# Decoder layer on one core: the second product of both FFNs by one level of Strassen's method, chained in PSUM

## The chip, the cores and the metric

The kernel runs on one core of one Trainium2 chip. The metric is the device time of one execution in microseconds (us), the median over several runs; lower is better. All inputs and the output are float32 in DRAM, and one launch computes the whole layer.

## The reference

One layer on a sequence of 512 tokens of width 1024: two SwiGLU FFNs with a hidden width of 2816, a token mixing between them (HGRN2 heads and causal pooling), a cross-attention into 256 memory tokens, and a layer norm after each of the four. What the change touches is the product with `w_out`:

```python
def _layernorm(x, g, b):
    ...
    return ((xf - mu) * lax.rsqrt(var + LN_EPS) * g + b)

def _swiglu(h, w_in, w_out):
    gate, up = jnp.split(h @ w_in, 2, axis=-1)      # w_in [1024, 5632]
    return (jax.nn.silu(gate) * up) @ w_out         # w_out [2816, 1024]

h = _layernorm(ALPHA * h + 0.5 * _swiglu(h, w_ffn1_in, w_ffn1_out), ln1_g, ln1_b)
h = _layernorm(ALPHA * h + _parallel_mixer(h, ...), ln2_g, ln2_b)
h = _layernorm(ALPHA * h + _memory_attention(h, mem, ...), ln3_g, ln3_b)
h = _layernorm(ALPHA * h + 0.5 * _swiglu(h, w_ffn2_in, w_ffn2_out), ln4_g, ln4_b)
```

## The kernel before

**Arithmetic.** Every large product is taken three times. An operand is split into two exact parts of type float32r, hi and lo: ScalarE (ACT) writes hi with a cast (L59), VectorE (DVE) subtracts it from the source and writes lo (L60). `mm3` (L53 to 56) then adds hi·hi, hi·lo and lo·hi in one PSUM bank. So a weight block of 128x1024 costs one DMA of 512 KB (L65), one cast of 128x1024 on ACT, one subtraction of 128x1024 on DVE, and its matmuls on TensorE (PE). Of the three matmuls on a tile the third is the first that reads the weight's lo part in `proj_T`; in the token-major products it is the second.

**Memory.** A DMA lands in `raw`, a ring of 3 buffers of the pool `wp`. The split halves of a weight go to the tags `whi` and `wlo` of the same pool, 4 buffers each (L70, L71), which nothing else uses but the first loads of x. The pool `big` has 15 slots of 8 KB per partition (`b8`, L44), which hold the activations; the last 4 weight blocks of an output product also go there (`stay`, L67). PSUM has 6 banks `mm` and 2 banks `tr`.

**First product of an FFN** (`ffn`, L239 to 265). It is feature-major: for each of the 22 column tiles j, `proj_T` (L220) makes the gate `pg` and the value `pu`, each [128 columns, 512 tokens], by 8x3 matmuls of 128x512. `glu` takes Silu of `pg` on ACT (L244), multiplies by `pu` from PSUM on DVE (L245) and splits the product into the tiles `f1g`/`f2g` (L247). Where a phase starts with the output of a layer norm, `proj_T2` (L228) makes two column tiles in halves of 256 tokens, so that the first half can start before the last tokens are normed.

**Second product** (`out_gemm`, L171 to 217). It is token-major: for each half of 512 output columns (hf) and each of 4 token tiles (t), 22 contraction tiles x 3 matmuls of 128x512 (L191 to 193) go into one PSUM bank: 2x4x22x3 = 528 matmuls for each FFN. The last blocks of a half are kept so that the token tiles end one after another. Then DVE adds the bank to the residual `h` (L204), takes the statistics (L207), and `ln_tile` (L141) norms the tile: bn_aggr (L144), variance plus eps (L146), a power on GpSimd (POOL, L148), and four DVE passes over 128x512 (L151, L154). `transpose_h` (L158) turns the normed tile by 8 PE transposes `trh`, and ACT and DVE split the result into the tiles `f1T` for the next phase.

**Order of the work.** Tile places the instructions of the program on each engine's queue, and each engine works through its queue in order. A tile of a pool can be written once the last reader of its slot is done, so the sizes of the pools decide how far ahead of its use on PE a weight's cast and subtraction stand in the queues of ACT and DVE. SyncE (SP) issues all DMAs.

Of the kernel before, what the change touches and what calls it, by code (L numbers as in the profile page):

```python
# [9 lines left out]
F32 = mybir.dt.float32  # L10
# [6 lines left out]
P = 128  # L17
# [6 lines left out]
H = 4  # L24
# [9 lines left out]
def layer_kernel(ctx: ExitStack, tc: tile.TileContext, a, out):  # L34
    nc = tc.nc
    const = ctx.enter_context(tc.tile_pool(name="const", bufs=1))
    big = ctx.enter_context(tc.tile_pool(name="big", bufs=15))
    wp = ctx.enter_context(tc.tile_pool(name="wp", bufs=4))
    res = ctx.enter_context(tc.tile_pool(name="res", bufs=1))
# [23 lines left out]
    def wblock(src, name, stay=False):  # L63
        raw = wp.tile([P, 1024], F32, tag="raw", name=f"raw_{name}", bufs=3)
        nc.sync.dma_start(raw, src)  # L65
# [19 lines left out]
    for k in range(KT):  # L85
# [3 lines left out]
        hi = wp.tile([P, 512], F32R, tag="whi", name=f"whix{k}")  # L89
        lo = wp.tile([P, 512], F32R, tag="wlo", name=f"wlox{k}")  # L90
# [25 lines left out]
    # lower bound of the forget gate: softmax over the two rows, first row  # L116
# [17 lines left out]
    def ln_bcast(g, b):  # L134
        G = sm.tile([P, D], F32, tag="G", name="G", bufs=1)
        B = sm.tile([P, D], F32, tag="B", name="B", bufs=1)
# [34 lines left out]
    def out_gemm(wsrc, nkt, act, alpha, g, b, eps, name, final=False, order=None, head0=None):  # L171
# [7 lines left out]
        for hf in range(2):  # L179
# [19 lines left out]
            ws = [wblock(wsrc[hf, order[i]], f"{name}{hf}_{i}", stay=hf == 1) for i in range(head, nb)]  # L199
# [28 lines left out]
    def proj_T2(ws, X, name):  # L228
        """Two column tiles at the start of a phase: the first half of the tokens goes first."""
# [8 lines left out]

    def ffn(win, wout, X, g, b, name, final, first=None):  # L239
        gt = [b8([P, 2, 2, S], F32R, f"{name}g{q}") for q in range(FT // 2)]  # L240

        def glu(j, pg, pu):
            sg = sm.tile([P, S], F32, tag="sg", name=f"{name}sg")
            nc.scalar.activation(sg, pg, AF.Silu)  # L244
            nc.vector.tensor_tensor(out=sg, in0=sg, in1=pu, op=ALU.mult)  # L245
            T = gt[j // 2]
            split(sg, T[:, j % 2, 0, :], T[:, j % 2, 1, :])  # L247

        j0 = 0
        if first is not None:  # L250
            for j, (pg, pu) in enumerate(first):
                glu(j, pg, pu)
            j0 = len(first)
        for j in range(j0, FT):
            ws = [wblock(win[j], f"{name}g{j}"), wblock(win[FT + j], f"{name}u{j}")]
            if j == 0:
                pg, pu = proj_T2(ws, X, f"{name}p")
            else:
                pg = proj_T(ws[0], X, name=f"{name}pg")
                pu = proj_T(ws[1], X, name=f"{name}pu")  # L260
            glu(j, pg, pu)
            if first is not None and 4 <= j < 4 + NT:
                nc.sync.dma_start(h[j - 4], a["x"][(j - 4) * P:(j - 3) * P, :])
# [393 lines left out]
```

## Time and profile before

| What | Value |
|---|---|
| Median of 3 runs | 1105.2 us (1104.76 to 1105.24) |
| The profiled execution's span, first to last instruction | 1103.7 us |
| Mean granted TensorE clock | 0.998 |
| PE busy | 1093.7 us of it |
| DVE, ACT, POOL busy | 498.7, 324.6, 41.5 us |
| DMA traffic | 113.59 MB, mean 103 GB/s |

The profile is one execution, recorded by the hardware. Its span is 1.5 us less than the median time, which counts what lies around the first and last instruction too. Busy times overlap. PE is busy when a matmul is in its pipeline; since matmuls overlap there, the start-to-start distance of two matmuls, not the duration shown for one, is what one of them costs. The span's other views are a list of instructions grouped by line and shape, a list of waits, the chain of work that ended last, and a timeline.

### The profile page before, as it was taken

Reading aid. Unit: us, or ns where it says so; the run is one execution under the profiler, and the core shown is the slowest. Engines: PE = TensorE matmul, PEld = TensorE weight load, DVE = VectorE, ACT = ScalarE, POOL = GpSimd, SP = SyncE. Lnnn points to the kernel's source line nnn. Section 1 sums busy time; section 2 is a strip of 40 time slices with the busy share of each in tenths; the row PEclk is TensorE's granted clock in tenths of the full one; section 3 lists DMA queues with packets and bytes.
Section 4 is the critical chain, followed back from the end, with each engine's and each line's share of the span. In section 5 each row is a group of like instructions: output and inputs, shape, how many; then the busy total and the mean of one; then the engine's idle time right before and its main releaser. Section 6 shows DMA issues by size and latency. Waiting matters only on the chain.

```text
span 1103.7 us, 12966 instructions
## 1 busy us (share of the span) xinstructions
PE 1093.7 (99%) x5318; PEld 921.4 (83%) x5318; DVE 498.7 (45%) x794; ACT 324.6 (29%) x490; POOL 41.5 (4%) x46
## 2 busy tenths in 40 slices
PE   9999999999999999999999999999999999999997
PEld 8888888888888988889889888888888888888885
DVE  5433333332344623775776456674333333322426
ACT  5322222221131332224424344223222222221210
POOL 0000000000000120311010000010000000000001
PEclk9999999999999999999999999999999999999999
DMA  7622222232242222111415421412222222222212
GB/s 260 237 96 96 96 96 96 95 120 100 96 154 94 77 96 77 58 66 60 156 54 175 149 77 39 153 39 97 98 101 102 99 97 96 96 96 96 96 58 76
DMA packets 34473, 113.59 MB, mean 103 GB/s; under 512 B 4336, under 2 KB 5616, under 8 KB 34416
## 3 DMA queue, kind: packets, MB, share of 16 engines
q1 hardware_dynamic: 34416, 112.78, 29.4%
q8 instruction: 41, 0.67, 0.2%
q14 instruction: 16, 0.13, 0.0%
HBM read 110.67 MB, written 2.10 MB: 102 GB/s over the span
## 4 chain that ended last, share of the span: by engine, by line
PE 99%; DVE 1%; ACT 0%; issue 0%; DVEq 0%; ACTq 0%
PE f1ps L192 4%; PE f1ps L191 4%; PE f2ps L193 4%; PE f2ps L191 4%; PE f1ps L193 4%; PE f2ps L192 4%; PE f2pg L54 3%; PE f2pu L54 3%; PE f2pu L56 3%; PE f2pg L56 3%; PE f2pg L55 3%; PE f2pu L55 3%; PE f1pg L55 3%; PE f1pu L55 3%; PE f1pu L56 3%; PE f1pg L56 3%
## 5 line engine op out<-in xcount | busy, mean ns | idle before, releaser
L60 DVE TENSOR_TENSOR wlo_f<-raw_f,whi_f 128x1024 fp32r<-128x1024 f32 x36 | 44.1, 1225 | 113.2 <-ACT whi_f L59 112.6
L59 ACT CAST whi_f<-raw_f 128x1024 fp32r<-128x1024 f32 x36 | 37.9, 1052 | 151.2 <-PE f2ps L193 60.1
L55 PE MATMUL f2pg<-xoT,whi_f2g 128*128 128x512 f32 x168 | 65.4, 389 | 0.0
L54 PE MATMUL f2pg<-xoT,whi_f2g 128*128 128x512 f32 x168 | 65.4, 389 | 0.0
L55 PE MATMUL f2pu<-xoT,whi_f2u 128*128 128x512 f32 x168 | 65.4, 389 | 0.0
L56 PE MATMUL f2pu<-xoT,wlo_f2u 128*128 128x512 f32 x168 | 65.4, 389 | 0.0
L54 PE MATMUL f2pu<-xoT,whi_f2u 128*128 128x512 f32 x168 | 65.4, 389 | 0.0
L56 PE MATMUL f2pg<-xoT,wlo_f2g 128*128 128x512 f32 x168 | 65.4, 389 | 0.0
L56 PE MATMUL f1pu<-xT,wlo_f1u 128*128 128x512 f32 x160 | 62.3, 389 | 0.0
L55 PE MATMUL f1pg<-xT,whi_f1g 128*128 128x512 f32 x160 | 62.3, 389 | 0.0
L55 PE MATMUL f1pu<-xT,whi_f1u 128*128 128x512 f32 x160 | 62.3, 389 | 0.0
L54 PE MATMUL f1pu<-xT,whi_f1u 128*128 128x512 f32 x160 | 62.3, 389 | 0.0
L54 PE MATMUL f1pg<-xT,whi_f1g 128*128 128x512 f32 x160 | 62.3, 389 | 0.0
L56 PE MATMUL f1pg<-xT,wlo_f1g 128*128 128x512 f32 x160 | 62.3, 389 | 0.0
L60 DVE TENSOR_TENSOR wlo_f2g<-raw_f2g,whi_f2g 128x1024 fp32r<-128x1024 f32 x22 | 27.0, 1226 | 74.1 <-ACT whi_f2g L59 74.1
L193 PE MATMUL f2ps<-whi_f,f2g 128*128 128x512 f32 x144 | 56.0, 389 | 0.0
L193 PE MATMUL f1ps<-whi_f,f1g 128*128 128x512 f32 x144 | 56.0, 389 | 0.0
L192 PE MATMUL f2ps<-wlo_f,f2g 128*128 128x512 f32 x144 | 56.0, 389 | 0.0
L191 PE MATMUL f1ps<-whi_f,f1g 128*128 128x512 f32 x144 | 56.0, 389 | 0.0
L192 PE MATMUL f1ps<-wlo_f,f1g 128*128 128x512 f32 x144 | 56.0, 389 | 0.0
L191 PE MATMUL f2ps<-whi_f,f2g 128*128 128x512 f32 x144 | 56.0, 389 | 0.0
L60 DVE TENSOR_TENSOR wlo_f1g<-raw_f1g,whi_f1g 128x1024 fp32r<-128x1024 f32 x20 | 24.5, 1226 | 65.7 <-ACT whi_f1g L59 65.6
(287 smaller groups left out, 2524.2 us busy)
## 6 DMA issues: line engine op xcount, KB each, us to landing
raw_f<-in_w1out SPq DMA_DIRECT2D x22, 512.0 KB, 3.5
raw_f2g<-in_w2in SPq DMA_DIRECT2D x22, 512.0 KB, 3.5
raw_f2u<-in_w2in SPq DMA_DIRECT2D x22, 512.0 KB, 3.5
raw_f<-in_w2out SPq DMA_DIRECT2D x22, 512.0 KB, 3.5
raw_f1g<-in_w1in SPq DMA_DIRECT2D x20, 512.0 KB, 3.5
raw_f1u<-in_w1in SPq DMA_DIRECT2D x20, 512.0 KB, 3.5
rawx<-in_first SPq DMA_DIRECT2D x16, 256.0 KB, 3.7
raw_wk<-in_wk SPq DMA_DIRECT2D x8, 512.0 KB, 3.5
```

The costliest lines, as they stand in the source:

```text
L54: nc.tensor.matmul(o, lh, rh, start=first, stop=False)
L55: nc.tensor.matmul(o, lh, rl, start=False, stop=False)
L56: nc.tensor.matmul(o, ll, rh, start=False, stop=last)
L59: nc.scalar.copy(out=hi, in_=src)
L60: nc.vector.tensor_tensor(out=lo, in0=src, in1=hi.bitcast(F32), op=ALU.subtract)
L191: nc.tensor.matmul(ps[t], ah[:, tsl], wh, start=i == 0 and j == 0, stop=False)
L192: nc.tensor.matmul(ps[t], ah[:, tsl], wl, start=False, stop=False)
L193: nc.tensor.matmul(ps[t], al[:, tsl], wh, start=False, stop=i == nb - 1 and j == 1)
```

## The change

For both FFNs, `ffn` is written anew and no longer calls `out_gemm`. With A the gated activations [512 tokens, 2816], cut in halves of the tokens and of the contraction (A11 to A22), and B the weight `w_out` cut in halves of the contraction and of the columns (B11 to B22), the product is made by seven products of half size instead of eight (Strassen's method in the form of Winograd): `a11b11, s1t1, s2t2, a12b21, s3t3, s4b22, a22t4`. Each runs over 11 contraction tiles and 2 token tiles, 3 matmuls of 128x512 each: 7x11x2x3 = 462 matmuls for each FFN. They run on six PSUM banks u, v, w (x 2 token tiles) which are not cleared between products that share a bank (`bank`), and DVE adds each bank into `h` as it stands after each product (`goes`, L351 and L353).

- **Left sums.** `glu` multiplies the two halves of the tokens apart and writes float32 (L281), 4 products of 128x256 for each pair of column tiles k and 11+k; four sums of 128x256 on GpSimd follow (`left_sums`, L286 to 289). All 77 operands of 128x256 stand in ten slots `f1a0` to `f1a9` of `big` and are split later, four at a time, into `f1l` (20 splits).
- **Right sums.** For each k, two rows of tiles of `w_out` are loaded (L265, `f1r`), four sums of 128x512 are made on GpSimd (L270, `f1t`), and GpSimd's own queue writes each to a scratch in DRAM (L271): 44 sums and 44 DMAs of 256 KB for each FFN. The second product loads them as weights, two DMAs of 256 KB for each block (`w_f1o0` to `w_f1o38`).
- **Memory.** `big` has 20 slots instead of 15. The tags `whi`, `wlo` and the two tiles of layer norm factors are gone: all split weights (`w_...`) take a slot of `big`, as does `GB`. This holds for all phases of the kernel.
- **Start of a phase.** In the second FFN and in the token mixing (`pf`), `proj_T2` now makes four column tiles by halves of 256 tokens, not two: 96 matmuls of 128x512 become 192 of 128x256. The sums of the first half of tokens are normed and transposed after `s4b22` (`finish`), those of the second after `a22t4`, the last product.

The diff, cut to its core:

```diff
-    big = ctx.enter_context(tc.tile_pool(name="big", bufs=15))
+    big = ctx.enter_context(tc.tile_pool(name="big", bufs=20))
...
-    def wblock(src, name, stay=False):
...
-        if stay:
-            both = b8([P, 2, 1024], F32R, f"ws_{name}")
-            hi, lo = both[:, 0, :], both[:, 1, :]
-        else:
-            hi = wp.tile([P, 1024], F32R, tag="whi", name=f"whi_{name}")
-            lo = wp.tile([P, 1024], F32R, tag="wlo", name=f"wlo_{name}")
-        split(raw, hi, lo)
-        return hi, lo
+    def wblock(src, name):
+        raw = wp.tile([P, 1024], F32, tag="raw", name=f"raw_{name}", bufs=3)
+        parts = src if isinstance(src, list) else [src]
+        n = 1024 if not isinstance(src, list) else 512
+        for i, part in enumerate(parts):
+            nc.sync.dma_start(raw[:, i * n:(i + 1) * n], part)
+        n *= len(parts)
+        both = b8([P, 2, 1024], F32R, f"w_{name}")
+        split(raw[:, :n], both[:, 0, :n], both[:, 1, :n])
+        return both[:, 0, :], both[:, 1, :]
...
     def ffn(win, wout, X, g, b, name, final, first=None):
...
+        ac = [b8([P, 8, 256], F32, f"{name}a{q}") for q in range(-(-NS // 8))]
...
+        def right_sums(k):
+            raw = b8([P, 2, 1024], F32, f"{name}r{k}")
+            for half in range(2):
+                nc.sync.dma_start(raw[:, half, :], wout[half * KH + k])
+            b11, b12, b21, b22 = raw[:, 0, :512], raw[:, 0, 512:], raw[:, 1, :512], raw[:, 1, 512:]
+            t = b8([P, 4, 512], F32, f"{name}t{k}")
+            for i, (p, x, y) in enumerate((("s1t1", b11, b12), ("s2t2", t[:, 0, :], b22),
+                                           ("s3t3", b12, b22), ("a22t4", t[:, 1, :], b21))):
+                nc.gpsimd.tensor_tensor(out=t[:, i, :], in0=x, in1=y, op=ALU.add)
+                nc.gpsimd.dma_start(sums[p][k], t[:, i, :])
...
+            for th in range(2):
+                sl = slice(th * 256, (th + 1) * 256)
+                nc.vector.tensor_tensor(out=dst[th], in0=sg[:, sl], in1=pu[:, sl], op=ALU.mult)
...
+        def operands(i):
+            q = i // 4
+            if q not in lsplit:
+                n = min(4, NS - 4 * q)
+                lt = b8([P, 2, 4, 256], F32R, f"{name}l{q}")
+                split(ac[q // 2][:, (q % 2) * 4:(q % 2) * 4 + n, :], lt[:, 0, :n, :], lt[:, 1, :n, :])
+                lsplit[q] = lt
+            r = i // 2
+            if r not in rsplit:
+                rsplit[r] = wblock([right(PROD[x // KH], x % KH) for x in (2 * r, 2 * r + 1) if x < NS], f"{name}o{r}")
...
+            for j, (x, y) in enumerate(((lh, rh), (lh, rl), (ll, rh))):
+                nc.tensor.matmul(o, x[:, tsl], y, start=opens and j == 0, stop=ends and j == 2, skip_group_check=True)
...
+            for i in range(lo_, min(hi_, tail)):
+                for ti in range(2):
+                    part(i, ti)
+            for ti in range(2):
+                for i in range(max(lo_, tail), hi_):
+                    part(i, ti)
+                after(p, ti)
+                if p == "s4b22":
+                    finish(ti)
+                if p == "a22t4":
+                    finish(2 + ti)
...
-    pf01 = proj_T2([wblock(a["wmix"][FF_ + hd], f"wf{hd}") for hd in range(2)], X1, "pf")
+    pfs = proj_T2([wblock(a["wmix"][FF_ + hd], f"wf{hd}") for hd in range(H)], X1, "pf")
```

How the queues change at three places. The first is DVE's queue in the first product of FFN 1. `wlo_f1g6` is the lo part of the weight of the gate of column tile 6, the L245 rows are the products of `glu`. Before:

```order
L245 TENSOR_TENSOR f1sg_446<-f1sg_446,f1pu_421 128x512
L60 TENSOR_TENSOR wlo_f1u5_528<-raw_f1u5_525,whi_f1u5_527 128x1024
L60 TENSOR_TENSOR f1g1_297<-f1sg_446,f1g1_297 128x512
L60 TENSOR_TENSOR wlo_f1g6_590<-raw_f1g6_587,whi_f1g6_589 128x1024
L245 TENSOR_TENSOR f1sg_513<-f1sg_513,f1pu_488 128x512
L60 TENSOR_TENSOR wlo_f1u6_596<-raw_f1u6_593,whi_f1u6_595 128x1024
```

In the changed kernel, around the step from k = 1 (column tiles 1 and 12; `f1pu_429` is the value of 12) to k = 2 (its gate's weight is `w_f1g2`):

```order
L61 TENSOR_TENSOR w_f1u12_426<-raw_f1u12_424,w_f1u12_426 128x1024
L281 TENSOR_TENSOR f1a0_290<-f1sg_389,f1pu_364 128x256
L281 TENSOR_TENSOR f1a21_391<-f1sg_389,f1pu_364 128x256
L281 TENSOR_TENSOR f1a4_294<-f1sg_454,f1pu_429 128x256
L281 TENSOR_TENSOR f1a8_298<-f1sg_454,f1pu_429 128x256
L61 TENSOR_TENSOR w_f1g2_476<-raw_f1g2_474,w_f1g2_476 128x1024
```

Before, the lo part of a gate's weight stood one product ahead of the `glu` that comes before its use on PE. Now it stands behind both halves of the `glu` of `f1pu_429`, which PE makes just before it uses `w_f1g2`. The same stands at k = 0 to 1, 2 to 3 and 6 to 7, and at the same four steps in FFN 2; at the other steps the split stands ahead of the `glu`.

The second is PE's queue where the second product of FFN 1 ends and the first normed tiles are turned (`trh00` and `trh01` read tile 0, `trh10` and `trh11` tile 1). Before, where `f1ps11` is the bank of the next token tile:

```order
L191 MATMUL f1ps11_2028<-ws_f11_9_2241,f1g9_305 128x512
L192 MATMUL f1ps11_2028<-ws_f11_9_2241,f1g9_305 128x512
L193 MATMUL f1ps11_2028<-ws_f11_9_2241,f1g9_305 128x512
L163 MATMUL trh00_2285<-ident_264,h0_292 128x128 x4
L163 MATMUL trh01_2294<-ident_264,h0_292 128x128 x4
L191 MATMUL f1ps11_2028<-ws_f11_10_2246,f1g10_306 128x512
```

In the changed kernel, between the last matmuls of `s4b22` (bank v, `f1v0`, `f1v1`) and the first of `a22t4` (bank u):

```order
L345 MATMUL f1v0_1909<-w_f1o32_2444,f1l16_2438 128x512 x3
L345 MATMUL f1v1_1910<-w_f1o32_2444,f1l16_2438 128x512 x3
L163 MATMUL trh00_2471<-ident_258,h0_286 128x128 x4
L163 MATMUL trh01_2480<-ident_258,h0_286 128x128 x4
L163 MATMUL trh10_2501<-ident_258,h1_287 128x128 x4
L163 MATMUL trh11_2510<-ident_258,h1_287 128x128 x4
L345 MATMUL f1u0_1794<-w_f1o33_2522,f1l16_2438 128x512
```

Before, the turning of tile 0 stood among the last matmuls of tile 1. Now all four stand straight behind the last matmul of both tiles, with no product between, and the first matmul of `a22t4` behind them. DVE's queue a little later at the same place in the changed kernel (the L61 rows with `f1T` are splits of turned tiles):

```order
L61 TENSOR_TENSOR f1T1_1787<-trh00_2471,f1T1_1787 128x2x128
L61 TENSOR_TENSOR f1T2_1788<-trh01_2480,f1T2_1788 128x2x128
L154 SCALAR_TENSOR_TENSOR h1_287<-h1_287,rstd_2495,GB_1783 128x512
L61 TENSOR_TENSOR f1T3_1789<-trh01_2480,f1T3_1789 128x2x128
L61 TENSOR_TENSOR f1T0_1786<-trh10_2501,f1T0_1786 128x2x128
L61 TENSOR_TENSOR w_f1o33_2522<-raw_f1o33_2519,w_f1o33_2522 128x1024
L61 TENSOR_TENSOR f1T1_1787<-trh10_2501,f1T1_1787 128x2x128
```

Ahead of these rows stand, from the end of `s4b22` on, the sums of v into `h0` and `h1`, two statistics, the norm of tile 0 and most of that of tile 1. The weight `w_f1o33` of `a22t4` is split behind all of them. In FFN 2, which has nothing to turn after its norm, the splits of `w_f2o33` to `w_f2o37` stand ahead of the norm.

The third is DVE's queue in the levels of the HGRN heads (L385 before, L515 now: eight predicated copies from PSUM at each level), where PE's projections `pv` of the pooling fill the waits. Before, the splits of the pooling's weights all stand ahead of the second level:

```order
L396 TENSOR_TENSOR KR_2467<-KR_2467,T0_2468 128x512
L60 TENSOR_TENSOR wlo_wv0_3234<-raw_wv0_3231,whi_wv0_3233 128x1024
L60 TENSOR_TENSOR wlo_wg0_3316<-raw_wg0_3313,whi_wg0_3315 128x1024
L385 COPY_PREDICATED scT_2781<-masks_266,lv2_3026 128x32x2 x8
L340 TENSOR_TENSOR ed_3021<-pl3_3014,recip_268 128x16
```

In the changed kernel, from the third level on:

```order
L526 TENSOR_TENSOR KR_2691<-KR_2691,Tlev_3203 128x128x4
L515 COPY_PREDICATED scT_3045<-masks_260,lv4_3387 128x16x4 x8
L525 TENSOR_TENSOR QP_2690<-QP_2690,Tlev_3203 128x128x4
L526 TENSOR_TENSOR KR_2691<-KR_2691,Tlev_3203 128x128x4
L61 TENSOR_TENSOR w_wv1_3408<-raw_wv1_3406,w_wv1_3408 128x1024
```

The weights of the last two pooling projections, and those of the gates `wg` after them, are now split inside the chain of the levels.

More of the change, by code (lines that the diff above doesn't have):

```diff
@@ new lines, in part @@
+        def part(i, ti):
+            p, k = PROD[i // KH], i % KH
+            o = ps[bank[p], ti]
+            lh, ll, rh, rl = operands(i)
+            tsl = slice(ti * P, (ti + 1) * P)
+            opens = k == 0 and p in ("a11b11", "s1t1", "a12b21")
+            ends = k == KH - 1 and p in ("a22t4", "s4b22", "a12b21")
+            for j, (x, y) in enumerate(((lh, rh), (lh, rl), (ll, rh))):
+                nc.tensor.matmul(o, x[:, tsl], y, start=opens and j == 0, stop=ends and j == 2, skip_group_check=True)
@@ new lines, in ffn, with finish, after @@
+        done = {"a12b21": 0, "s4b22": 1, "s3t3": 1, "a22t4": 0}
+        def finish(t):
+            ln_tile(t, stats[t], GB, 4.0 * LN_EPS)
+            if final:
+                for q in range(2):
+                    nc.sync.dma_start(out[t * P:(t + 1) * P, q * 512:(q + 1) * 512], h[t][:, q * 512:(q + 1) * 512])
+            else:
+                transpose_h(t, tiles)
+        def after(p, ti):
+            for t0, hf, scaled, op in goes[p]:
+                t = t0 + ti
+                into(t, hf, ps[bank[p], ti], scaled, op)
+                if p in done:
+                    nc.vector.bn_stats(stats[t][:, hf, :], h[t][:, hf * 512:(hf + 1) * 512])
```

114 lines of the change are left out of this document (83 added, 31 removed).

## The prediction

> **What bounds the kernel now.** First the page: busy times, granted clock, and the chain that ended last.
>
> ```profile
> span 1103.7 us, 12966 instructions
> PE 1093.7 (99%) x5318; PEld 921.4 (83%) x5318; DVE 498.7 (45%) x794; ACT 324.6 (29%) x490; POOL 41.5 (4%) x46
> PEclk9999999999999999999999999999999999999999
> GB/s 260 237 96 96 96 96 96 95 120 100 96 154 94 77 96 77 58 66 60 156 54 175 149 77 39 153 39 97 98 101 102 99 97 96 96 96 96 96 58 76
> PE 99%; DVE 1%; ACT 0%; issue 0%; DVEq 0%; ACTq 0%
> ```
>
> PE is busy 99% of the span at full clock, and 99% of the last chain is PE. DVE, ACT and the DMA have room on the mean. Then the waits of PE (engine, line, releaser; us, times, longest).
>
> ```profile
> PE idle L83 <- DVE mhalf L107: 1.0, 1, 1.0
> PE po L54 <- ACT PT L59: 0.6, 1, 0.6
> ```
>
> PE waits 1.6 us in all. So before, each matmul taken away is time won, and each new wait of PE is time lost, one for one. The forecast is a balance of these two.
>
> **What a matmul costs.** The timeline gives starts. Six steps of 128x512 and six of 128x256:
>
> ```profile
> 1072.66 0.39 PE L192 MATMUL f2ps<-wlo_f,f2g 128*128 128x512 f32 x1
> ...
> 1074.02 0.39 PE L192 MATMUL f2ps<-ws_f,f2g 128*128 128x512 f32 x1
> ```
>
> ```profile
> 742.81 0.28 PE L55 MATMUL f2p<-xoT,whi_f2g 128*128 128x256 f32 x1
> ...
> 743.53 0.28 PE L55 MATMUL f2p<-xoT,whi_f2g 128*128 128x256 f32 x1
> ```
>
> (1074.02 - 1072.66) / 6 = 0.227 us, and (743.53 - 742.81) / 6 = 0.120 us. Strassen takes 2 x (528 - 462) = 132 matmuls of 128x512 away: -132 x 0.227 = -29.9 us. The wider start of two phases turns 96 of 128x512 into 192 of 128x256: 192 x 0.120 - 96 x 0.227 = +1.3 us. **PE's work falls by 28.6 us.** It could only be less if a matmul into a bank that other products have opened cost more; no row suggests it.
>
> **What the order of the queues adds.** These groups (mean ns of one behind the busy time) price the steps:
>
> ```profile
> L60 DVE TENSOR_TENSOR wlo_f<-raw_f,whi_f 128x1024 fp32r<-128x1024 f32 x36 | 44.1, 1225 | 113.2 <-ACT whi_f L59 112.6
> L59 ACT CAST whi_f<-raw_f 128x1024 fp32r<-128x1024 f32 x36 | 37.9, 1052 | 151.2 <-PE f2ps L193 60.1 <-PE f1ps L193 56.1 <-issue 15.6
> L60 DVE TENSOR_TENSOR xoT<-trh,xoT 128x256 fp32r<-128x256 f32 x16 | 6.4, 422 | 3.5 <-ACT xoT L59 3.3
> L59 ACT CAST oT<-po 128x512 fp32r<-128x512 f32 x8 | 4.6, 596 | 8.0 <-PE po L56 8.0
> L395 DVE TENSOR_TENSOR QP<-QP,Tlev 128x512 f32<-128x512 f32 x12 | 8.4, 696 | 0.0
> ```
>
> *First, the steps of the GLU.* At four steps in each FFN the lo part of the next gate's weight is made behind the last `glu`. When PE ends the value `f1pu`, DVE has two products of 128x256 to do (0.42 each; the row nearest to them is `xoT<-trh`, which reads PSUM too) and then the subtraction, 1.23. PE has two matmuls that need only hi, 0.45. A handoff is read at the end of the kernel:
>
> ```profile
> 1095.33 0.39 PE L193 MATMUL f2ps<-ws_f,f2g 128*128 128x512 f32 x1
> 1095.76 0.69 DVE L204 SCALAR_TENSOR_TENSOR h<-h,f2ps 128x512 f32<-128x512 f32 x1 [0.94 <-PE f2ps L193]
> ```
>
> DVE starts 0.43 us after the last matmul's start, 0.2 more than its 0.227. So PE waits 0.84 + 1.23 + 0.2 - 0.45 = 1.8 us, and eight times that is **+14.5 us**. Its lower end is 8 x 1.2 (products at half the price), the upper 8 x 2.2 (at 0.69 for a half, the price of 128x512).
>
> *Second, the hole at the end of FFN 1.* The norm of one tile, from the sum to the last pass (the last column is idle time of the engine and its releaser):
>
> ```profile
> 1090.32 0.69 DVE L204 SCALAR_TENSOR_TENSOR h<-h,f2ps 128x512 f32<-128x512 f32 x1 [0.94 <-PE f2ps L193]
> 1091.04 0.69 DVE L207 BATCH_NORM_STATS2 stats<-h 128x6 f32<-128x512 f32 x1
> 1091.77 0.21 DVE L144 BATCH_NORM_AGGREGATE mv<-stats 128x2 f32<-128x12 f32 x1
> 1092.01 0.15 DVE L146 TENSOR_SCALAR ve<-mv 128x1 f32<-128x1 f32 x1
> 1092.08 1.41 DVE L151 SCALAR_TENSOR_TENSOR h<-h,mv,G 128x512 f32<-128x512 f32 x2
> 1093.40 1.41 DVE L154 SCALAR_TENSOR_TENSOR h<-h,rstd,B 128x512 f32<-128x512 f32 x2
> ```
>
> That is 0.69 + 0.69 + 0.21 + 0.15 + 1.41 + 1.41 = 4.56 us for a tile. Before, PE had the next tile's matmuls meanwhile. Now the queue of PE holds nothing between the end of `s4b22` and the turning of tiles 0 and 1, and `a22t4` waits behind that for `w_f1o33`. DVE does two norms (9.1), five splits of turned halves (5 x 0.42) and the subtraction of `w_f1o33` (1.23): 12.4 us. From it go 0.68, by which tile 0 ends before tile 1 (three matmuls), the 0.45 that PE has in hand, and the turning itself, which PE did before too:
>
> ```profile
> 352.82 1.38 PE L163 MATMUL trh<-ident,h 128*128 128x128 f32 x8
> 353.96 0.48 PE L191 MATMUL f1ps<-ws_f,f1g 128*128 128x512 f32 x1
> ```
>
> Eight take 353.96 - 352.82 = 1.14, so 16 take 2.3. With a handoff: 12.4 + 0.2 - 0.7 - 0.45 - 2.3 = 9.2. Right behind come three more turned splits, the left split `f1l17` and `w_f1o34`, 3 x 0.42 + 2 x 1.23 = 3.7 us, against ten matmuls and two, 2.7: 1.0 more. **+10.2 us**, in FFN 1 alone: FFN 2 splits its weights ahead of the norm and turns nothing.
>
> *Third, token mixing and attention.* Their split weights had 4 buffers of their own and now share the 20 slots with long-lived tiles, so many stand behind work that waits for PE. The clearest: `w_wv10` behind the eviction of the bank `vm01`. ACT evicts (0.60), casts the weight (1.05), DVE subtracts (1.23), with a handoff 3.1 us, and PE has one matmul, 0.23: 2.8. Summed likewise, each less what PE still has: `w_wf3` behind the last norm 3.0, `w_wq1` and the diagonal behind `pq` 2.6, the keys and states 4.1, `w_wk5` 3.4, `w_wxq30` 0.7, `w_xo0_0` 1.4; with the first, 18.0. In the levels
>
> ```profile
> 450.28 1.30 DVE L385 COPY_PREDICATED scT<-masks,lv 128x64 f32<-128x64 int32 x8
> ```
>
> a level's half is 1.30 + 2 x 0.70 = 2.7 us of DVE, and the lo parts of `w_wv1`, `w_wv0` and three gates stand behind such halves: 4 matmuls of PE (0.9) against 2.7, then about 2 for `w_wv0`, and less later, 4.6 in all. **+22.6 us.** This is the softest term: PE's other work there is counted by the pitches above, and the small matmuls between may take longer and hide it. Its ends are 0 and 30.
>
> **Sum.** 1103.7 - 28.6 + 14.5 + 10.2 + 22.6 = 1122.4 us of span; the median lies 1.5 above the span: **1124**.
>
> *A clock that falls in the hole* is set at nothing, since no row shows PE idle for so long. The start shows slow matmuls:
>
> ```profile
> 5.48 0.63 PE L55 MATMUL first<-xT,whix 128*128 128x512 f32 x1
> 5.91 0.63 PE L54 MATMUL first<-xT,whix 128*128 128x512 f32 x1
> ...
> 7.37 0.39 PE L54 MATMUL first<-xT,whix 128*128 128x512 f32 x1
> ```
>
> The step is 0.43 there and 0.23 from 7.37 on. A like stretch of 2.5 us behind the hole would cost 2.5 x (1 - 0.227 / 0.43) = 1.2 us, which I keep for the range. The Trainium skill (page "TensorE: Matmul & The Clock Gate", section "Part 1: The HAM clock gate") states that the clock halves after an idle window of about 3.4 us and returns after about 3.4 us of activity. By it the estimate would be 3.4 x 0.47 = 1.6 us more, 1126.
>
> **The rivals.**
>
> *The saving comes through (faster).* The third term doesn't appear, because PE comes to those places later than the pitches say and the splits are ready. For it: in token mixing PE's small matmuls are the least well counted. Against it: PE waited there for nothing before, with the splits well ahead; ahead is what they no longer are. It decides where the third term falls under 28.6 - 24.7 = 3.9 us; at zero the time is 1105.2 - 28.6 + 24.7 = 1101, and with the first term at its lower end (9.6) and the hole at 8, 1094. Chance 0.24.
>
> *GpSimd sets the pace of the first product.* Its sums stand behind each `glu`, and slots of weights wait for its DMAs. The rows nearest:
>
> ```profile
> L337 POOL TENSOR_TENSOR pl<-pl 128x512 f32<-128x512 f32 x10 | 14.3, 1433 | 64.8 <-ACT pl L332 64.4
> raw_f<-in_w1out SPq DMA_DIRECT2D x22, 512.0 KB, 3.5
> rawx<-in_first SPq DMA_DIRECT2D x16, 256.0 KB, 3.7
> ```
>
> For each k, 4 x 1.43 + 4 x 0.72 = 8.6 us, and 4 DMAs, whose issue on GpSimd no row shows: between 0 and 3.5 us each. PE needs 96 x 0.227 = 21.8 for a k. Only at the upper end, 22.6, does GpSimd decide: + 22 x 0.8 = 18, 1142. Chance 0.08. The Trainium skill (page "DMA: Bandwidth & Descriptors", section "Anatomy of one DMA — SWDGE (gpsimd) path") fits 2.0 us + bytes / 436e3 to such a DMA. By it the estimate is 2.6 us each, 19.0 for a k, and the sum stays.
>
> *The weights come too slowly in the second product.* A block served 24 matmuls (5.4 us); now it serves 12 (2.7). The ring of 3 turns in 3.5 + 1.5 x (1.05 + 1.23) = 6.9, 2.3 for a block (the half for the left split). If the turn takes 9 us, 3.0: + 78 x 0.28 = 22, 1146. Against it: the start moved 260 GB/s in such pieces, and 512 KB in 2.7 us is 194. Chance 0.11.
>
> **How the numbers follow.** The forecast has 0.57. A measurement of this kernel can tell 0.2%, 2.2 us, from no change. Faster by more is nearly all of the first rival, 0.23; no change is a third term within 2 us of 3.9, 0.05 (a sliver of that rival and of the forecast); the rest is slower, 0.72. The range goes from 1094, the first rival's low end, to 1146, the last rival's; the forecast alone, with the third term from 10 to 30, has 1111 to 1131.
>
> **What would show it.** In the profile after: 924 matmuls of the second products at a step of 0.227; waits of PE for DVE at the lo part of `w_f1g2` and its seven likes, 1.8 us each; one idle stretch of PE of some 9 us with the 16 turnings in it, ahead of `a22t4` in FFN 1 and none such in FFN 2; waits of 1 to 3 us at `w_wf3`, `w_wk`, `w_wv10` and in the levels. Wrong it is if PE's waits sum to less than 28 us, or if they are for DMAs or GpSimd.

## The result, and the profile after

The changed kernel takes **1151.4 us** (median of 4 runs, 1149.0 to 1153.1), the kernel before 1105.0 beside it: ratio 1.042, 95% interval [1.040, 1.043]. It is slower, as forecast, but by 46 us and not by 19, and outside the forecast's range. The profiled run took 1149.0 and has a span of 1147.2 us.

The page of the changed kernel: span, busy times, granted clock in 40 slices, GpSimd's own DMA queue (packets, MB, share), and the last chain by engine.

```profile
span 1147.2 us, 13808 instructions
PE 1085.0 (95%) x5282; PEld 906.4 (79%) x5282; DVE 576.2 (50%) x880; ACT 369.6 (32%) x520; POOL 296.8 (26%) x310
PEclk9999999998998999999999999999999999989998
q0 software_dynamic: 7040, 23.07, 5.3%
PE 75%; POOL 7%; DMA 7%; DVE 5%; issue 3%; ACT 2%; SPq 0%; DVEq 0%; ACTq 0%; POOLq 0%
```

PE's busy time fell by only 8.7 us though 28.6 us of matmuls went: busy time also grows where the clock is lower. No engine has taken PE's place as the busiest; the last chain, once 99% PE, now runs a quarter of the time through other engines and DMAs: GpSimd (POOL) and DMAs 7% each, DVE 5%. The waits of PE tell where:

```profile
PE f1u L345 <- ACT w_f1o L60: 8.2, 1, 8.2
PE f2u L345 <- ACT w_f2o L60: 7.8, 1, 7.8
PE f2pg L57 <- DVE w_f2g L61: 7.0, 5, 1.6
PE f1pg L57 <- DVE w_f1g L61: 6.5, 6, 1.7
PE trh L163 <- DVE h L154: 4.3, 1, 4.3
PE pk L55 <- ACT w_wk L60: 2.8, 3, 1.6
PE dg L425 <- ACT QP L416: 2.0, 1, 2.0
PE f1pg L55 <- ACT w_f1g L60: 2.0, 2, 1.1
PE trh L163 <- issue: 1.7, 2, 1.5
PE vm L634 <- ACT w_wv L60: 1.6, 1, 1.6
```

The rows of `f1pg` and `f2pg` are the waits in the GLU; those on DVE are at their longest as the forecast has its steps (1.6 and 1.7 us for 1.8). `trh` is the hole, `pk`, `dg` and `vm` the late splits of token mixing and attention. The two longest stand nowhere in the forecast: PE waits 8 us at the first matmul of each second product.

**A balance of PE's steps.** The list shows only single long waits, so I went through the starts of all PE matmuls. A step from one start to the next has a usual length for its shape, 0.227, 0.120 or 0.11 us. The sum of these is the work; what a step has above it is idle time, or, in stretches in which all steps take twice as long, loss to the clock. The remainder is what lies ahead of the first and behind the last matmul.

| us | Work | Idle | Clock | Remainder | Span |
|---|---|---|---|---|---|
| Before | 1086.4 | 7.9 | 0 | 9.4 | 1103.7 |
| After | 1057.7 | 67.2 | 9.9 | 12.4 | 1147.2 |
| After, less forecast | -0.1 | +12.0 | +9.9 | +3.0 | +24.8 |

The work fell by 28.7 (forecast 28.6). Idle time rose by 59.3, for which the forecast had 14.5 + 10.2 + 22.6 = 47.3. By place it rose by 21.0 in the GLU steps, 17.6 at the starts of the two second products, 6.9 in the hole, 14.2 in mixing and attention, and -0.3 at the start.

**The 8 us at the start of the second product.** The timeline of the changed kernel there, from three engines (start, duration; idle time before and its releaser in brackets):

```profile
247.50 2.54 POOL L270 TENSOR_TENSOR f1t<-f1r 128x512 f32<-128x512 f32 x2 [8.67 <-DMA f1r<-in_w1out]
...
256.62 0.56 POOL L271 DMA_DIRECT2D f1a22t<-f1t  x1 [0.30 <-POOL f1t L270]
...
263.35 1.99 ACT L60 CAST w_f1o<-raw_f1o 128x1024 fp32r<-128x1024 f32 x2 [21.84 <-DMA f1a22t<-f1t]
...
264.44 0.79 PE L345 MATMUL f1u<-w_f1o,f1l 128*128 128x512 f32 x1 [8.19 <-ACT w_f1o L60]
```

ACT has been idle for 21.84 us ahead of the cast of the first `w_out` weight, because the slot that this weight takes in `big` belongs to the last `f1t`, whose fourth sum leaves by a DMA that GpSimd issued at 256.62. The cast starts 6.7 us after that. GpSimd itself waited 8.67 us for a load, `f1r`, which needs a slot of the same pool.

This write lands later than others of its kind. The one of the group before was issued at 232.56, and the cast that waited for it started at 235.04, 2.5 us later. At the last group SyncE issues two loads of the layer norm factors `GB` within 0.3 us of the write, and from 258 to 260 us the DMA engines are 97% busy (window shown below):

```profile
256.35 0.33 SPq L137 DMA_DIRECT2D GB<-in_ln_g  x1
256.73 0.42 SPq L138 DMA_DIRECT2D GB<-in_ln_b  x1
```

FFN 2 has the same meeting: loads at 1021.21 and 1021.59, the write at 1021.48, the cast at 1027.77, where the group before has 997.40 and 999.87. So some 4 of the 8 us at each start may come from the write sharing the DMA engines with these loads. That is not shown, since no run moves the loads alone.

### The profile page after: what moved, and what is told of

Its sections match the earlier page's. It is cut to its first block, busy times and chain, and to the rows that moved or that the text cites. A ratio compares the mean times of both kernels' runs of the same rounds, so it can differ in the third digit from the quotient of the medians.

```text
span 1147.2 us, 13808 instructions
## 1 busy us (share of the span) xinstructions
PE 1085.0 (95%) x5282; PEld 906.4 (79%) x5282; DVE 576.2 (50%) x880; ACT 369.6 (32%) x520; POOL 296.8 (26%) x310
## 4 chain that ended last, share of the span: by engine, by line
PE 75%; POOL 7%; DMA 7%; DVE 5%; issue 3%; ACT 2%; SPq 0%; DVEq 0%; ACTq 0%; POOLq 0%
PE f1u L345 6%; PE f2u L345 5%; PE f2v L345 3%; PE f1v L345 3%; PE f2pg L57 2%; PE f1pg L57 2%; PE f2pu L57 2%; PE f1pu L55 2%; PE f2pu L55 2%; PE f1pu L56 2%; PE f1pu L57 2%; PE f2pu L56 2%; POOL f2t L270 2%; POOL f1t L270 2%; PE f1pg L55 2%
## 5 line engine op out<-in xcount | busy, mean ns | idle before, releaser
L345 PE MATMUL f1u<-w_f1o,f1l 128*128 128x512 f32 x264 | 64.4, 404 | 8.7 <-ACT w_f1o L60 8.2
L345 PE MATMUL f2u<-w_f2o,f2l 128*128 128x512 f32 x264 | 62.5, 397 | 8.2 <-ACT w_f2o L60 7.8
L57 PE MATMUL f2pg<-xoT,w_f2g 128*128 128x512 f32 x160 | 63.0, 394 | 7.0 <-DVE w_f2g L61 7.0
L57 PE MATMUL f1pg<-xT,w_f1g 128*128 128x512 f32 x160 | 63.0, 394 | 6.5 <-DVE w_f1g L61 6.5
L345 PEld LDWEIGHTS f1u<-w_f1o,f1l 128*128 128x128 f32 x264 | 51.4, 196 | 21.4 <-ACT w_f1o L60 9.1
L61 DVE TENSOR_TENSOR w_f2g<-raw_f2g,w_f2g 128x1024 fp32r<-128x1024 f32 x22 | 32.1, 1459 | 68.6 <-ACT w_f2g L60 68.4
L345 PEld LDWEIGHTS f2u<-w_f2o,f2l 128*128 128x128 f32 x264 | 50.5, 192 | 19.7 <-ACT w_f2o L60 8.2
L61 DVE TENSOR_TENSOR w_f1o<-raw_f1o,w_f1o 128x1024 fp32r<-128x1024 f32 (+1 forms) x39 | 46.8, 1206 | 36.5 <-ACT w_f1o L60 36.3
L55 PE MATMUL f1pg<-xT,w_f1g 128*128 128x512 f32 x160 | 62.7, 392 | 2.0 <-ACT w_f1g L60 2.0
L61 DVE TENSOR_TENSOR w_f2o<-raw_f2o,w_f2o 128x1024 fp32r<-128x1024 f32 (+1 forms) x39 | 47.2, 1215 | 33.3 <-ACT w_f2o L60 33.1
L61 DVE TENSOR_TENSOR w_f1g<-raw_f1g,w_f1g 128x1024 fp32r<-128x1024 f32 x20 | 27.9, 1396 | 70.4 <-ACT w_f1g L60 70.1
L55 PE MATMUL f2pg<-xoT,w_f2g 128*128 128x512 f32 x160 | 62.4, 390 | 0.9 <-ACT w_f2g L60 0.9
L56 PE MATMUL f2pg<-xoT,w_f2g 128*128 128x512 f32 x160 | 62.3, 390 | 0.0
L56 PE MATMUL f1pg<-xT,w_f1g 128*128 128x512 f32 x160 | 62.3, 389 | 0.0
L55 PE MATMUL f1pu<-xT,w_f1u 128*128 128x512 f32 x160 | 62.2, 389 | 0.0
L56 PE MATMUL f1pu<-xT,w_f1u 128*128 128x512 f32 x160 | 62.2, 389 | 0.0
L55 PE MATMUL f2pu<-xoT,w_f2u 128*128 128x512 f32 x160 | 62.2, 389 | 0.0
L56 PE MATMUL f2pu<-xoT,w_f2u 128*128 128x512 f32 x160 | 62.2, 389 | 0.0
L57 PE MATMUL f2pu<-xoT,w_f2u 128*128 128x512 f32 x160 | 62.2, 389 | 0.0
L57 PE MATMUL f1pu<-xT,w_f1u 128*128 128x512 f32 x160 | 62.2, 389 | 0.0
```

What stands on the lines that cost most here:

```text
L55: nc.tensor.matmul(o, lh, rh, start=first, stop=False)
L56: nc.tensor.matmul(o, lh, rl, start=False, stop=False)
L57: nc.tensor.matmul(o, ll, rh, start=False, stop=last)
L61: nc.vector.tensor_tensor(out=lo, in0=src, in1=hi.bitcast(F32), op=ALU.subtract)
L345: nc.tensor.matmul(o, x[:, tsl], y, start=opens and j == 0, stop=ends and j == 2, skip_group_check=True)
```

## The experiments

Two theories stood to begin with. *Slots* (theory A in what follows): with all split weights in `big`, a weight's cast and subtraction queue behind whatever frees its slot; the idle time is that, and the forecast only mis-sized it. *GpSimd* (theory B): its sums and DMAs for the right operand delay slots and DVE, which the forecast had as a rival and priced at nothing unless GpSimd's throughput decided.

**e1: the pool without Strassen.** The kernel before with the changed kernel's memory:

```diff
-    big = ctx.enter_context(tc.tile_pool(name="big", bufs=15))
+    big = ctx.enter_context(tc.tile_pool(name="big", bufs=20))
...
+        both = b8([P, 2, 1024], F32R, f"w_{name}")
+        hi, lo = both[:, 0, :], both[:, 1, :]
```

and likewise for the first loads of x and the layer norm factors.

> The kernel before, with nothing of Strassen: only its split weights and the layer norm factors are put into the 20 slots of the shared pool, as the changed kernel does. Theory A (the time goes to weights that are split too late because they wait for a slot of the shared pool and so stand behind work that waits for PE): the queue of DVE then has both splits behind the glu at every second column tile, 10 steps in FFN 1 and 11 in FFN 2, some 1.8 us each, and the same late splits in token mixing and attention as the changed kernel (its PE is idle there 14 us more than before, with 3 us at half clock): about 1105 + 38 + 17 = 1160 us. Theory B (the time goes to GpSimd: its sums, its DMAs and the slots that wait for them): no GpSimd work is added, so about 1105 us.

Measured: 1214.1 us (1208.5 to 1216.6), ratio 1.098 [1.095, 1.101]. Its page and the longest waits of PE:

```profile
span 1212.1 us, 12959 instructions
PE 1136.3 (94%) x5318; PEld 935.9 (77%) x5318; DVE 497.3 (41%) x794; ACT 325.6 (27%) x490; POOL 37.6 (3%) x46
```

```profile
PE f2pg L54 <- ACT w_f2g L59: 26.9, 11, 2.4
PE f1pg L54 <- ACT w_f1g L59: 25.9, 11, 2.4
```

The same arithmetic with the same matmuls, only with other slots, costs 109 us: 83.5 of idle time and 25.4 of clock in the balance. That is 54 us above theory A's time. In mixing and attention the idle time rises by 12.8 us, close to the 14.2 of the change, so that term is the pool's. In the first product it is 33.2 and 35.7 us, more than in the changed kernel: PE waits 2.4 us for a gate's cast at 11 steps in each FFN. What a pool of 20 costs depends on who else lives in it, so this number can't be carried over to the change.

**e2: the right sums left out.** No load of `w_out` ahead, no sums on GpSimd, no DMAs of them; the four products that would read them read tiles of `w_out` instead, so the result isn't the layer's.

```diff
-            if p in sums:
-                return sums[p][k]
-            half, col = {"a11b11": (0, 0), "a12b21": (1, 0), "s4b22": (1, 1)}[p]
+            half, col = {"a11b11": (0, 0), "a12b21": (1, 0), "s4b22": (1, 1),
+                         "s1t1": (0, 1), "s2t2": (0, 1), "s3t3": (1, 1), "a22t4": (1, 0)}[p]
...
-            right_sums(k)
```

> The changed kernel without the right sums: w_out is not loaded a first time, GpSimd makes no right sums and issues no DMA, and the second product reads tiles of w_out where it would read sums (so the right sums are left out of what is computed). PE's work and the shared pool stay. Theory A: the late splits of the GLU, the norm's hole and token mixing stay; only the wait at the start of both second products (8 us each), the half clock behind it and the 3 us that GpSimd takes to close its queue at the end go: about 1125 to 1130 us. Theory B: nearly all of the loss goes, about 1080 to 1090 us.

Measured: 1115.9 us (1115.3 to 1118.8), ratio 1.010 [1.009, 1.012]: 35.5 us less than the changed kernel. The waits at the start of both second products are gone, and those of the GLU are smaller:

```profile
PE f2pg L57 <- DVE w_f2g L61: 4.6, 4, 1.1
...
PE f1pg L57 <- DVE w_f1g L61: 3.5, 3, 1.3
```

That is between the times of the two theories. So the right sums cost some 35 us, though GpSimd's busy time is a quarter of the span. Whether it is the sums, the traffic or the DMAs that GpSimd issues stayed open.

**e3: a ring of their own for the weights.** The changed kernel with

```diff
-    both = b8([P, 2, 1024], F32R, f"w_{name}")
+    both = wp.tile([P, 2, 1024], F32R, tag="w", name=f"w_{name}", bufs=4)
```

(the first loads of x too) and 16 slots in `big` instead of 20.

> The changed kernel with the split weights back in a ring of their own, 4 buffers of 8 KB, and 16 shared slots instead of 20 (the same memory); all sums and DMAs on GpSimd stay. Theory A: the splits of the GLU and of token mixing stand ahead again and w_f1o0 needs no slot that a GpSimd DMA still reads; left are part of the norm's hole (about 5 us), some half clock, and the 3 us at the end: 1105 - 28.6 + 3 + 5 + 5 = about 1088 us. Theory B: GpSimd's work is as before, so it stays above 1125 us.

Measured: 1121.5 us (1119.3 to 1123.6), ratio 1.015 [1.013, 1.016], 29.9 less than the changed kernel, but 33 above theory A's time. Mixing and attention fell to 7.6 us idle in the balance (before: 5.3). But in each FFN one wait of 13 us has come up in the first product, at k = 10, the last:

```profile
PE f1pg L55 <- ACT w_f1g L60: 13.0, 1, 13.0
PE f2pg L55 <- ACT w_f2g L60: 12.7, 1, 12.7
```

Its timeline on ACT tells why:

```profile
233.38 1.04 ACT L60 CAST f1l<-f1a 128x1024 fp32r<-128x1024 f32 x1 [26.42 <-DMA f1a22t<-f1t]
234.82 1.03 ACT L60 CAST w_f1g<-raw_f1g 128x1024 fp32r<-128x1024 f32 x1
```

The weight of the gate needs no slot of `big` any more, but it stands in ACT's queue behind the first left split `f1l`, which does, and that slot again goes free by a DMA that GpSimd issued (at 226.65, again beside the loads of `GB`, at 226.38 and 226.75). The wait of the changed kernel has only moved.

**e5: the turning of tiles 0 and 1 put later**, behind the matmuls of `a22t4` that both its token tiles take in turn and those that its first token tile takes alone, the norms where they were:

```diff
-                    finish(ti)
+                    finish(ti, False)
...
+                if p == "a22t4" and not final and ti == 0:
+                    for t in range(2):
+                        transpose_h(t, tiles)
```

> The changed kernel with one edit: in FFN 1 the turning of tiles 0 and 1 is placed behind the matmuls of a22t4 that both token tiles share, instead of straight behind s4b22. Theory A: the norm's hole of about 7 us of PE and the 10 us at half clock behind it (about 4 us lost) go: about 1141 us. If the norm only moves its cost (DVE late for w_f1o33 instead), 1147 us or more.

Measured: 1140.4 us (1136.4 to 1140.9), ratio 1.031 [1.029, 1.033]. The `trh` rows are gone from the waits, the rest stays (`f1u` 8.9, `f2u` 8.3). The hole is worth 11.0 us by the medians, 8.0 by the spans of the two profiles (the profiled run of the changed kernel is the fastest of its four).

**e12: the same right sums, written by SyncE's queue.** The changed kernel with one edit:

```diff
-                nc.gpsimd.dma_start(sums[p][k], t[:, i, :])
+                nc.sync.dma_start(sums[p][k], t[:, i, :])
```

> The changed kernel with one edit: SP issues the 88 writes of the right sums instead of GpSimd; shared slots and queues of weights stay as they are. Theory A in its present form (late splits and slots, with GpSimd's DMAs as a smaller part: 3 us at the end, subtractions of 128x1024 that take 1.9 us instead of 1.2 while GpSimd issues a DMA, and the wait of w_f1o0 for a slot): 3 us at the end and some 5 to 10 us more go, 1138 to 1144 us. If GpSimd's DMAs were the larger part, under 1120 us.

Measured: 1123.4 us (1119.5 to 1123.6), ratio 1.016 [1.014, 1.017]. The engine that issues 88 DMAs is worth 28.1 us, more than I expected, with the same sums, bytes and slots. From the issue to the landing of the same transfer, first in the changed kernel and then in this one (KB each and median us at the end):

```profile
f1a22t<-f1t POOLq DMA_DIRECT2D x11, 256.0 KB, 5.3
```

```profile
f1a22t<-f1t SPq DMA_DIRECT2D x11, 256.0 KB, 2.1
```

The other three of a group go from 3.0, 2.4 and 2.6 to 2.0 us. And at the start of the second product, in e12:

```profile
246.27 0.32 SPq L271 DMA_DIRECT2D f1a22t<-f1t  x1
...
248.47 2.00 ACT L60 CAST w_f1o<-raw_f1o 128x1024 fp32r<-128x1024 f32 x2 [10.31 <-DMA f1a22t<-f1t]
```

The last sum is sent 10.4 us earlier than in the changed kernel (246.27 for 256.62), since loads, sums and DMAs follow each other through the slots, and the cast starts 2.2 us after it instead of 6.7. The write also stands ahead of the loads of `GB` now (the first at 246.69), in one queue with them. PE, which is ready 3.3 us earlier (252.7 for 256.1), no longer waits there. In the balance against the changed kernel idle time is 22.8 us lower (17.6 at these starts, 5.0 in the GLU steps), the clock 3.3, the remainder 3.3.

**e14: both edits**, e3's ring and e12's queue.

> The kernel of e3_own4 (weights in a ring of their own) with the edit of e12_after_sp (SP writes the right sums): the fourth corner of the square of these two edits. If the two causes are apart, the gains add: 1121.5 - 28 = about 1093 us. If both mostly remove the same waits (slots that wait for GpSimd's DMAs), the gain is smaller: the 13 us wait of e3_own4 at the last step of each GLU shrinks but stays in part, and the norm's hole stays: 1097 to 1108 us.

Measured: **1086.7 us** (1085.0 to 1087.6), ratio **0.983** [0.982, 0.985]: 18.3 us faster than the kernel before, with the changed kernel's arithmetic.

```profile
span 1083.2 us, 13723 instructions
PE 1067.7 (99%) x5282; PEld 902.8 (83%) x5282; DVE 583.5 (54%) x880; ACT 372.9 (34%) x520; POOL 261.4 (24%) x222
```

```profile
PE trh L163 <- DVE h L154: 2.6, 1, 2.6
PE trh L163 <- issue: 2.5, 1, 2.5
PE idle L83 <- DVE mhalf L107: 1.1, 1, 1.1
```

| Median us | GpSimd writes | SyncE writes |
|---|---|---|
| Weights in `big` | 1151.4 | 1123.4 |
| Weights in a ring of 4 | 1121.5 | 1086.7 |

Alone, the edits bring 29.9 and 28.1; together 64.8, 6.8 more than their sum. The wait at k = 10 of e3 ended with a DMA of GpSimd, and it goes with the second edit. Of PE's waits little but the hole is left (the rows not shown are 0.6 and less), and the balance has 14.0 idle, 1.9 clock and 9.6 remainder: 1103.7 - 28.7 + 6.1 + 1.9 + 0.2 = 1083.2.

**e6, e8 and e10: the left splits in the ring too, and the turning spread over `a22t4`.** e6 is e3 with

```diff
-                lt = b8([P, 2, 4, 256], F32R, f"{name}l{q}")
+                lt = wp.tile([P, 2, 4, 256], F32R, tag="w", name=f"{name}l{q}", bufs=4)
...
+            if p == "a22t4" and not final:
+                transpose_h(0, tiles)
...
+                if p == "a22t4" and not final and ti == 0:
+                    transpose_h(1, tiles)
```

> The kernel of e3_own4 with two more edits: the split left operands (f1l, f2l) take buffers of the weights' ring too, and the turning of tiles 0 and 1 of FFN 1 is spread among the matmuls of a22t4. In e3_own4 PE was idle 13 us at the last step of each GLU, since the first left split stood early in ACT's queue and waited for a slot that a GpSimd DMA still read, and 6 us in the norm's hole. Theory A: both go with the half clock behind them (26 + 5 + 6 + 2 us); 1121.5 - 36 or so: about 1085 us. Theory B (GpSimd itself is the bound somewhere): another wait for POOL takes its place, above 1100 us.

Measured: 1107.8 us (1105.8 to 1108.6), ratio 1.002 [1.001, 1.003], level with the kernel before. That is theory B's time without its sign, for PE has no wait for POOL. The 13 us at k = 10 are gone without touching GpSimd's queue, which agrees with the reading of e3. e8 adds the writes by SyncE to it; e10 leaves the right sums out of e6 (as in e2, its result isn't the layer's).

> The kernel of e6_own4_l with one edit: the 88 writes of the right sums are issued by SP instead of by GpSimd. The 3 us between the end of SP's work and GpSimd's answer at the end of the program should go if they belong to GpSimd's own DMA queue: 3 us less than e6_own4_l. If SP's queue, which then waits for GpSimd's sums with the loads of weights behind it, holds up weights, it is slower than e6_own4_l.

> The kernel of e6_own4_l without the right sums (no first load of w_out, no sums of it, no GpSimd DMAs; the second product reads tiles of w_out in their place, so the right sums are left out of what is computed). It shows what GpSimd's sums and writes still cost there. Theory A: only the 3 us at the end and a few waits, so 3 to 6 us under e6_own4_l, about 1080 us. Theory B: far under it, by 20 us or more.

Measured: e8 1096.1 us (1095.7 to 1097.4), ratio 0.992 [0.991, 0.994]; e10 1096.9 (1096.3 to 1098.0), 0.993 [0.991, 0.994]. With the writes on SyncE's queue the 88 sums, the early loads for them and their writes (23 MB each) cost nothing that shows; with GpSimd's queue they cost 11.7 (1107.8 - 1096.1), even without slots for weights to hold. But e8 is 9.4 slower than e14, so with that queue out of the way e6's other two edits do harm. e8's longest wait, 4.0 us, is in FFN 2, ahead of `a22t4`, where e14 has none. DVE and PE at that place in e8:

```profile
1066.35 1.41 DVE L154 SCALAR_TENSOR_TENSOR h<-h,rstd,GB 128x512 f32<-128x512 f32 x2
...
1067.79 1.17 DVE L61 TENSOR_TENSOR w_f2o<-raw_f2o,w_f2o 128x1024 fp32r<-128x1024 f32 x1
...
1069.01 11.10 PE L345 MATMUL f2u<-w_f2o,f2l 128*128 128x512 f32 x36 [4.02 <-DVE ve L146]
```

With the left splits in the ring, the weight of `a22t4` is split behind the last pass of a norm here too, and PE starts as it ends.

**e11: the norms spread as well**, e8 with the norms of tiles 0 and 1 put among the matmuls of `a22t4`, in both FFNs (the turning moves behind them too; not shown):

```diff
+                if p == "a22t4" and i - lo_ in (1, 3):
+                    finish((i - lo_) // 2, False)
...
-                if p == "s4b22":
-                    finish(ti, False)
```

> The kernel of e8_sp with one more edit, in both FFNs: the norms of tiles 0 and 1 are placed among the first matmuls of a22t4 instead of ahead of them, and the turning of tile 0 two steps later. In e8_sp PE still waited 5 us for w_f2o behind those norms, lost 3 us at half clock after it, and DVE was so late that the last norm started 2 us after its bank was ready. Theory A: these go, 1096 - 8 = about 1088 us. If DVE is simply full there, they only move: 1094 us or more.

Measured: 1096.8 us (1096.2 to 1097.1), ratio 0.993 [0.991, 0.994]: no gain over e8. The wait behind `ve` has become one for a weight, `f2u <- w_f2o` 4.5 us (2 times, longest 3.9): DVE has norms and splits to do in the same stretch, in whatever order.

**e9: five buffers in the ring**, e6 with `bufs=5` for the tag `w` and 15 slots in `big`:

```diff
-    big = ctx.enter_context(tc.tile_pool(name="big", bufs=16))
+    big = ctx.enter_context(tc.tile_pool(name="big", bufs=15))
```

> The kernel of e6_own4_l with 5 buffers in the weights' ring and 15 shared slots. Theory A: within 3 us of e6_own4_l, as few late splits are left in either. If the shared slots become too few, later sums and waits for POOL: slower by 5 us or more.

Measured: 1128.9 us (1127.3 to 1130.5), ratio 1.022 [1.020, 1.023], 21.1 slower than e6. Its waits lie all through the second products (`f2v <- w_f2o` 5.4, `f1v <- w_f1o` 4.2, `f2u <- w_f2o` 3.2). With both edits together, one slot less in `big` costs more than one weight further ahead gains; by which tile that comes was not taken apart.

## Why the prediction was right in sign and wrong in size

**The saving** of 28.6 us of PE work is right (28.7), and it is real: e14 keeps 18.3 of it.

**"GpSimd sets the pace of the first product" is the step that failed.** It was priced by throughput alone: sums and DMAs for a k against PE's 21.8 us, with 18 us lost only if a DMA held GpSimd for 3.5, and at 2.6 us each "the sum stays". As throughput that holds: in the changed kernel a DMA holds GpSimd for 0.56 us (the row of 256.62), and e8 and e10 show the sums to be free. But what a queue of its own costs is 28.1 us (e12), and throughput doesn't show the two ways in which it comes. (In the balance they are 22.6 and 3.3 us, with 3.3 of clock behind the waits.) By the sign that the prediction set itself it is wrong here: the two longest waits in PE's list, 16.0 of its 51 us, are for casts that a DMA of GpSimd released.

- *A slot stays taken until the DMA lands*, and others queue behind the slot. The prediction had named it ("slots of weights wait for its DMAs") and then priced only the pace. Load, sums, write and the next load that needs a slot form a loop, and at the end of the first product that loop is longer than PE's 21.8 us for a k: the last writes of the last three groups of FFN 1 are issued 23.9 and 24.1 us apart (208.63, 232.56, 256.62), in e12 19.4 and 21.0 (205.80, 225.23, 246.27). It costs 17.6 us at the starts of the second products and 5.0 in the GLU at k = 9 and 10. There the cast of a gate's weight waits for a slot until GpSimd has made its late sums, and the next cast until the write has landed (k = 10 of FFN 1):

```profile
232.29 1.04 ACT L60 CAST w_f1g<-raw_f1g 128x1024 fp32r<-128x1024 f32 x1 [16.48 <-POOL f1t L270]
...
235.04 1.05 ACT L60 CAST w_f1g<-raw_f1g 128x1024 fp32r<-128x1024 f32 x1 [0.27 <-DMA f1a22t<-f1t]
```

  The Trainium skill (page "DMA: Bandwidth & Descriptors", section "Anatomy of one DMA — SWDGE (gpsimd) path") has a fit by which the estimate for such a transfer is 2.6 us; the medians here were 2.4 to 5.3, the last of each group the slowest, and 2.0 to 2.1 from SyncE's queue.
- *The end of the program*, 3 us: below.

*DVE becomes slower while GpSimd works*, which the prediction didn't have either. The subtraction of a 128x1024 weight takes 1.22 us in the changed kernel when GpSimd does nothing (200 of them), 1.51 under one of its sums (44), and 1.85 when it issued a DMA meanwhile (14; in nearly all of these a sum began too). The longest, and what GpSimd did in it:

```profile
36.05 0.71 POOL L271 DMA_DIRECT2D f1s1t<-f1t  x1 [0.31 <-POOL f1t L270]
36.78 1.30 POOL L270 TENSOR_TENSOR f1t<-f1t,f1r 128x512 f32<-128x512 f32 x1
36.96 3.45 DVE L61 TENSOR_TENSOR w_f1u<-raw_f1u,w_f1u 128x1024 fp32r<-128x1024 f32 x1 [3.87 <-ACT w_f1u L60]
...
39.26 0.56 POOL L271 DMA_DIRECT2D f1s2t<-f1t  x1
```

With SyncE's queue (e12) the means are 1.22 and 1.6, and the third case is gone. The Trainium skill (page "GPSIMD Engine Reference", section "1. Specifications") says that GpSimd shares its interfaces to SBUF with VectorE, and that VectorE's instructions with two inputs there contend with it. The trace agrees, and gives the size. But no wait of PE is shown to hang on it: the subtractions that PE waits for in the GLU took 1.22 to 1.23 us (those that start at 52.30, 794.30 and 841.64), and with e12 these waits stay as they were.

**"A clock that falls in the hole is set at nothing"** failed too. The granted clock halved in five stretches, 30.7 us together, and cost 9.9; the 1.2 kept for the range was too little. Windows of 2 us in the changed kernel (us; busy time of PE, PEld, DVE, ACT, POOL; granted clock; DMA share; GB/s):

```profile
258.00:260.00 2.00, 0.00 (x0) 0.00 (x0) 0.00 (x0) 0.00 (x0) 0.00 (x0) 1.00 0.97 162
266.00:268.00 2.00, 2.00 (x5) 1.52 (x5) 2.00 (x3) 1.71 (x2) 1.60 (x1) 0.50 0.56 192
```

PE is idle at full clock first, and then does five matmuls in 2 us instead of nine, with PE shown as busy throughout: that is one reason why PE's busy time fell so little.

**The GLU steps** were forecast at 14.5. The GLU cost 21.0, of which 5.0 go with GpSimd's queue (e12 has 16.0). The mechanism is right, and the eight steps cost 1.9 to 2.0 us each in the balance for the 1.8 of the forecast. The rest are the late casts at k = 9 and 10 shown above, which wait for slots.

**The hole** was forecast at 10.2. Taking the turning out of it gains 8.0 to 11.0 (e5). That the sum fits is luck, for its parts don't: idle time is 6.9, and behind it comes a stretch of 10.2 us at half clock that was set at nothing. In e5 the clock is at half in five stretches too, 34.1 us together, so what e5 gains is idle time. The timeline of PE there:

```profile
360.97 1.97 PE L163 MATMUL trh<-ident,h 128*128 128x128 f32 x8 [4.26 <-DVE h L154]
364.39 1.09 PE L163 MATMUL trh<-ident,h 128*128 128x128 f32 x4 [1.45 <-issue]
366.88 2.48 PE L345 MATMUL f1u<-w_f1o,f1l 128*128 128x512 f32 x4
```

**Late splits in mixing and attention**, the softest term, were forecast at 22.6 and cost 14.2; e1 with 12.8 and e3 with 2.3 show them to come from the shared slots, as argued. Too large it was by 8.4.

Together, against the forecast span of 1122.4: starts +17.6, clock +9.9, GLU +6.5, remainder +3.0, mixing -8.4, hole -3.3, and -0.5 of small parts and rounding, +24.8. That e12 lies at 1123.4, near the forecast, is no confirmation: there a smaller third term and the clock cancel out.

Open is why the two edits of e14 bring 6.8 us more together than apart: that e3's wait hangs on GpSimd's DMA is shown, how much of the 6.8 it makes is not. Open too is how much of the wait at the second products' starts belongs to GpSimd's queue itself and how much to the loads of `GB` that meet its last write. A hole closed in e14 as in e5 was not run.

## What to carry to other kernels

A pool shared by weights that run ahead and by tiles that live long, or that leave by a DMA, sets where each weight's split stands in the in-order queues: give the weights a ring of their own and look at who frees the slot. An engine at a quarter of its time can still cost 28 us, by when its results land and not by how many it makes. A smaller product pays only if the feed stays ahead: the same arithmetic took 1151 us and 1087.

## What the runs showed of the hardware

- **The clock can halve after short pauses too.** PE waited 1.62 us from 634.4 and 0.53 us from 636.7, and from 636.9 to 640.3 the clock was at half:

```profile
634.00:636.00 2.00, 0.38 (x3) 0.03 (x1) 1.14 (x3) 1.61 (x3) 0.00 (x0) 1.00 0.01 4
638.00:640.00 2.00, 2.00 (x7) 1.51 (x6) 1.45 (x2) 0.00 (x0) 0.00 (x0) 0.50 0.81 270
```

  All stretches of the changed kernel last 3.4, 6.8 or 10.2 us, but for the one in which the program ends. Not every such pause does it: none of the eight GLU steps was followed by half clock. The Trainium skill (page "TensorE: Matmul & The Clock Gate", section "Part 1: The HAM clock gate") has the clock halve after an idle window of about 3.4 us and return after as much activity. The length of the stretches agrees; a wholly idle window of 3.4 us was not needed, and e1, whose longest pauses in the GLU are 2.4 us, has 15 stretches, 54.6 us in all, most of them there.
- **DMAs issued by GpSimd lengthen the end of the program.** The last pass of the last norm, in the changed kernel and in e12:

```profile
1139.32 1.41 DVE L154 SCALAR_TENSOR_TENSOR h<-h,rstd,GB 128x512 f32<-128x512 f32 x2
```

```profile
1113.21 1.41 DVE L154 SCALAR_TENSOR_TENSOR h<-h,rstd,GB 128x512 f32<-128x512 f32 x2
```

  In the changed kernel GpSimd's last DMA stands at 1021.48:

```profile
1021.48 0.56 POOL L271 DMA_DIRECT2D f2a22t<-f2t  x1 [0.30 <-POOL f2t L270]
```

  From the end of that pass to the end of the span it is 6.5 us in the changed kernel (span 1147.2) and 3.1 in e12 (span 1117.7); the kernel before has 3.4, e6 6.5, e8 3.1. The 3 us come and go with GpSimd's queue, although its last DMA was issued 118 us before that last pass.
